# Emptying PSUM banks in steps, adding the residual by DMA, and a fixed TensorE order behind a feed-forward output product

## The chip, the cores and the metric

The kernel is one program on one core of a Trainium2 chip. TensorE (PE) multiplies into eight PSUM banks of 128 x 512 float32; VectorE (DVE), ScalarE (ACT) and GpSimd (POOL) work beside it; SyncE (SP), ACT and POOL issue DMAs. Each engine takes its own instructions in order and waits on semaphores. The metric is the device time of one execution in microseconds, as the median of several runs. Lower is better.

## The reference

Two layers over 256 latent and 256 context tokens, width 1024, all float32. Layer 0 mixes tokens with an mLSTM, layer 1 with latent attention whose keys and values come from a small projection of context and latent tokens together. Behind each mixer comes a convolutional feed-forward block. The part that is changed lies between layer 0's feed-forward and layer 1's attention:

```python
f = _conv_ffn(_modulate(x, ml[3], ml[4]), ...)      # ... (silu(conv(gate)) * up) @ w_out
x = _layer_norm(ALPHA * x + ml[5] * f, ln_g[i, 1], ln_b[i, 1])
# the same for xc with mc; then layer 1:
hl = _modulate(x, ml[0], ml[1])
ckv, k_rope = jnp.split(h @ w_dkv, [A_KVLORA], axis=-1)          # for hc and for hl
kv = _rms_norm(ckv, kv_norm) @ w_ukv
```

## The kernel before, in words

Every float32 product is made of three float32r matmuls (`mm3`, lines 383 to 385): each operand is split into a rounded high part (ACT, line 323 or 388) and a low remainder (DVE, line 326 or 389).

*Weights.* `Stream` holds one list of all weight blocks in the order of use (`_plan`). A block of 128 x 1024 is loaded into a raw buffer (`_load`, by SP), split into a `w` buffer (three of them, `NB`) or, if marked wide, into two `u` tiles, and then used. `use` splits up to eight blocks ahead, as far as `limit` allows and a `w` buffer is free; `pump` does the same up to a given block. A raw buffer becomes free when its block has been split, and then the next load goes out. From block y22 on there are seven raw buffers. Blocks named yt4 are special: SP loads a stored sum (`t2d`, line 278) and POOL adds the weight to it by an accumulating DMA (line 279).

*The output product of layer 0's feed-forward* (`w_fout0`) is a Strassen-like scheme over two token groups (g 0 context, g 1 latent) and two column halves. Four products (yt2, y11, yt3, yt1) run together over six weight blocks and fill all eight PSUM banks (`p6, p1, p7, p5`). Then y21, y22 and yt4 follow, each into one pair of banks (`ps`, one bank for each half b of the 128-row blocks). Operands of the last three are reloaded from DRAM (`zr`, ACT queue) and split (`fz`) by `operand()`. The sums u1 to vv of the four products, gated, are the first part of the output; `add()` adds the gated later products, and bn_stats feed the layer norm. The residual x1 was written to DRAM by `ln_x` two stages earlier and is loaded into `z` (line 1414).

*Order.* A scheduler places the instructions of each engine by the program's order and its own estimate of when each is ready; `keep_in_program_order` (`pin`) holds one instruction behind all earlier ones of its engine. `self.bg` is a list of generators, of which `tick` runs one step.

Before, behind the four products, all banks are emptied at once (lines 1418 to 1434): ACT copies p1 to u1, DVE makes u2, u3, v, u4. `residual()` then multiplies by the gate (1441), adds ALPHA times z (1442), and for the last quarter takes statistics (1444). While yt4's first three blocks run, the context rows are normalised (`z_norm`) and transposed (`ln_T`); then `mid(None, ...)` makes the context's kv product (`mla_ctx`, three dkv blocks held), and only then come yt4's last three blocks (`YTAIL`), wide. The latent rows are normalised and transposed while `ukn` and `uv` use the context's kv; then `mla` begins with the latent kv product and goes on with dq. `PA, PB, PC` limit how far weights are split meanwhile.

Of the kernel before, what the change touches and what calls it, by code (L numbers as in the profile page):

```python
# [11 lines left out]
ALU = mybir.AluOpType  # L12
# [25 lines left out]
PA, PB, PC = 0, 2, 4  # L38
# [32 lines left out]
def _plan():  # L71
# [35 lines left out]
    for n in ("y21", "y22", "yt4"):  # L107
        for j in range(6):
            if (n, j) == ("yt4", 6 - YTAIL):
                for c, m in enumerate((3, 3, 2)):  # L110
                    add(("dkv", 0, c), m * 320)
            add((n, 0, j), cols[j], n == "yt4" and j >= 6 - YTAIL)
    for c in range(2):
        add(("ukn", 0, c), 1024, True)
# [240 lines left out]
class K:  # L355
# [861 lines left out]
    def ln_x(self, ln, zs, dst):  # L1217
# [134 lines left out]
    def w_fout0(self, x1d, mid):  # L1352
# [39 lines left out]
        n = 0  # L1392
        for i in range(6):
            for name, ps, x in (("yt2", p6, "S2"), ("y11", p1, "1"), ("yt3", p7, "S3"), ("yt1", p5, "S1")):
# [7 lines left out]
                if n >= 8:  # L1402
                    operand()
# [6 lines left out]
                if n >= 16 and n % 2 == 0:  # L1410
                    if n == 16:
                        z = []
                    t = self.uf("z")
                    nc.gpsimd.dma_start(t, x1d[len(z)])
                    z.append(t)
                n += 1
        stats = [self.tiny(12, "st").rearrange("p (a b) -> p a b", b=6) for _ in range(4)]
        u1, u3, u4, vv = [], [], [], []
        for b in range(2):
            u = self.s2("u1")  # L1420
            nc.scalar.copy(u, p1[b])
            u1.append(u)
            u = self.s2("u2")
            nc.vector.tensor_tensor(u, p6[b], u1[b], op=ALU.add)
            u4.append(u)
        for b in range(2):
            u = self.s2("u3")
            nc.vector.tensor_tensor(u, p7[b], u4[b], op=ALU.add)
            u3.append(u)
        for b in range(2):  # L1430
            v = self.s2("v")
            nc.vector.tensor_tensor(v, p5[b], u3[b], op=ALU.subtract)
            nc.vector.tensor_tensor(u4[b], p5[b], u4[b], op=ALU.subtract)
            vv.append(v)

        def residual():

            for us, g, c in ((u1, 0, lo), (u4, 0, hi), (u3, 1, lo), (vv, 1, hi)):
                for b in range(2):
                    zz = z[2 * g + b]  # L1440
                    nc.vector.tensor_tensor(us[b], us[b], gate[g][:, c], op=ALU.mult)
                    nc.vector.scalar_tensor_tensor(zz[:, c], zz[:, c], ALPHA, us[b], op0=ALU.mult, op1=ALU.add)
# [528 lines left out]
```

## Time and profile before

| | |
|---|---|
| median of 3 runs (lowest, highest) | 1388.25 us (1387.74, 1389.04) |
| profiled execution, its own time | 1389.13 us |
| span of that profile | 1387.4 us |
| TensorE busy | 1355.8 us, 98% of the span |
| VectorE, ScalarE, GpSimd busy | 77%, 50%, 9% |
| mean granted TensorE clock | 0.997 |
| DMA | 297.63 MB, mean 215 GB/s |

The profile comes from one execution. The span runs from its first to its last instruction; the execution's own time has some microseconds outside it. A busy TensorE is not TensorE at its peak, since matmuls overlap. Idle time of an engine is put down to what ended it; idle time of an engine that bounds nothing costs nothing. In rows of the windows the DMA share is the mean over the core's sixteen DMA engines. Times in rows count from the start of the span.

### The profile page before, as it was taken

The numbers are of one execution on the slowest core, as the hardware profiler recorded it, in microseconds if no ns is written. First come the engines' busy times: TensorE is split into PE (matmuls) and PEld (weight loads), VectorE is DVE, ScalarE is ACT, GpSimd is POOL, SyncE is SP. The second block draws the span as 40 slices with busy tenths as digits, with TensorE's granted clock in tenths as the row PEclk, the third lists the DMA queues.
The fourth block names the chain that finished last, engine by engine and source line by source line (L and its number), as shares of the span: only waits on it lengthen the run. The fifth ranks groups of instructions, "written<-read, shape, count | busy, mean of one in ns | idle before, by whom it ended". The sixth has DMA issues, their size and how long they took to land.

```text
span 1387.4 us, 19172 instructions
## 1 busy us (share of the span) xinstructions
PE 1355.8 (98%) x6903; PEld 1140.1 (82%) x6903; DVE 1075.0 (77%) x1726; ACT 699.2 (50%) x1179; POOL 121.2 (9%) x215
## 2 busy tenths in 40 slices
PE   7999999999999999999999999999999999999997
PEld 3788888888788888878798888888777898899986
DVE  6599757687688697788799878668898789777773
ACT  6585534435444545375643434334547567455560
POOL 0033000011011011120002000000001001000000
PEclk9999999999999999999999999999999999999999
DMA  9689847879666374766747877647987426367750
GB/s 339 217 292 325 289 152 248 237 261 326 210 205 203 104 231 140 242 196 223 242 143 242 295 234 234 211 148 234 310 224 224 137 99 207 116 188 230 209 183 31
DMA packets 97903, 297.63 MB, mean 215 GB/s; under 512 B 12136, under 2 KB 24808, under 8 KB 97808
## 3 DMA queue, kind: packets, MB, share of 16 engines
q1 hardware_dynamic: 68672, 218.52, 48.9%
q0 software_dynamic: 17472, 57.57, 13.4%
q10 hardware_dynamic: 11664, 20.32, 4.0%
q8 instruction: 54, 0.88, 0.3%
q14 instruction: 41, 0.34, 0.1%
HBM read 262.90 MB, written 33.46 MB: 214 GB/s over the span
## 4 chain that ended last, share of the span: by engine, by line
PE 86%; DVE 7%; DMA 3%; ACT 2%; issue 2%; ACTq 0%; SPq 0%; DVEq 0%
PE fin L383 9%; PE fin L384 9%; PE fin L385 9%; PE tok L383 6%; PE tok L385 6%; PE tok L384 6%; PE qk L383 4%; PE qk L384 4%; PE qk L385 4%; PE y L384 4%; PE y L385 4%; PE y L383 4%; PE up L383 2%; PE up L385 2%; PE up L384 2%
## 5 line engine op out<-in xcount | busy, mean ns | idle before, releaser
L326 DVE TENSOR_TENSOR w<-raw,w 128x1024 fp32r<-128x1024 f32 (+3 forms) x290 | 347.9, 1203 | 159.1 <-ACT w L323 158.3
L323 ACT CAST w<-raw 128x1024 fp32r<-128x1024 f32 (+3 forms) x290 | 300.3, 1037 | 331.6 <-PE fin L385 105.0
L384 PE MATMUL fin<-h,w 128*128 128x256 f32 (+1 forms) x696 | 231.7, 333 | 0.0
L385 PE MATMUL fin<-h,w 128*128 128x256 f32 (+1 forms) x696 | 231.4, 333 | 0.0
L383 PE MATMUL fin<-h,w 128*128 128x256 f32 (+1 forms) x696 | 231.2, 333 | 0.1
L512 DVE SCALAR_TENSOR_TENSOR junk<-ar,bc 128x1024 f32<-128x1024 f32 x128 | 155.9, 1218 | 4.9 <-ACT bc L554 2.3
L384 PEld LDWEIGHTS fin<-h,w 128*128 128x128 f32 x696 | 132.2, 190 | 13.0 <-DVE h L1212 0.2
L383 PEld LDWEIGHTS fin<-h,w 128*128 128x128 f32 x696 | 131.9, 190 | 13.2 <-ACT h L1211 0.3
L385 PEld LDWEIGHTS fin<-h,w 128*128 128x128 f32 x696 | 132.2, 190 | 12.7
L383 PE MATMUL qk<-xc,w 128*128 128x512 f32 x256 | 100.7, 393 | 0.0
L385 PE MATMUL qk<-xc,w 128*128 128x512 f32 x256 | 99.9, 390 | 0.0
L384 PE MATMUL qk<-xc,w 128*128 128x512 f32 x256 | 99.8, 390 | 0.0
L383 PEld LDWEIGHTS qk<-xc,w 128*128 128x128 f32 x256 | 48.1, 188 | 10.2 <-issue 0.4
L385 PEld LDWEIGHTS qk<-xc,w 128*128 128x128 f32 x256 | 48.1, 188 | 9.9
L384 PEld LDWEIGHTS qk<-xc,w 128*128 128x128 f32 x256 | 48.1, 188 | 9.6
L383 PE MATMUL up<-hT,w 128*128 128x512 f32 x128 | 50.5, 394 | 0.5 <-ACT hT L388 0.5
L384 PE MATMUL up<-hT,w 128*128 128x512 f32 x128 | 50.1, 392 | 0.4 <-DVE hT L389 0.4
L385 PE MATMUL up<-hT,w 128*128 128x512 f32 x128 | 50.1, 391 | 0.3 <-DVE w L389 0.3
L383 PE MATMUL tok<-w,hT 128*128 128x512 f32 x128 | 49.8, 389 | 0.0
L384 PE MATMUL tok<-w,hT 128*128 128x512 f32 x128 | 49.8, 389 | 0.0
L385 PE MATMUL tok<-w,hT 128*128 128x512 f32 x128 | 49.8, 389 | 0.0
L326 DVE TENSOR_TENSOR wu<-raw,wu 128x1024 fp32r<-128x1024 f32 (+1 forms) x33 | 39.1, 1200 | 8.2 <-ACT wu L323 7.9
(453 smaller groups left out, 3036.6 us busy)
## 6 DMA issues: line engine op xcount, KB each, us to landing
raw<-in_ws SPq DMA_DIRECT2D x287, 512.0 KB, 4.5
ar<-in_adaT SPq DMA_DIRECT2D x80, 512.0 KB, 4.7
adaw<-in_ada_w SPq DMA_DIRECT2D x32, 256.0 KB, 6.5
t2d<-raw ACTq DMA_DIRECT2D x13, 512.0 KB, 6.2
raw<-t2d SPq DMA_DIRECT2D x13, 512.0 KB, 6.3
raw<-in_ws POOLq DMA_DIRECT2D x13, 512.0 KB, 8.0
zr<-fd ACTq DMA_DIRECT2D x33, 128.0 KB, 3.2
xmd<-xr POOLq DMA_DIRECT2D x16, 256.0 KB, 5.4
```

The lines of the kernel that those rows point to most:

```text
L323: k.nc.scalar.copy(h[:, :cols], src)
L326: k.nc.vector.tensor_sub(l[:, :cols], src, h[:, :cols])
L383: mm(out, w[0], x[0], start=start, stop=False)
L384: mm(out, w[0], x[1], start=False, stop=False)
L385: mm(out, w[1], x[0], start=False, stop=stop)
L512: nc.vector.scalar_tensor_tensor(o, w, 1.0, self.bc[j], op0=ALU.mult, op1=ALU.mult, accum_out=col[:, k, j:j + 1])
```

## The change

Six things, all in the stretch described above:

1. u1 is copied from y11's banks right behind y11's last block, pinned, two products before the four end. `operand()` starts at block 6 instead of 8.
2. The sums are made in eight steps of a generator during y21 and y22.
3. x1 is stored already multiplied by ALPHA (`ln_x` has a factor). `z` is no longer loaded: the gated sum is written to it, and a POOL DMA adds x1 to it, half by half, eight of 128 x 512.
4. The dkv blocks stand behind all of yt4 in the list. Weights are split up to them, without PA to PC.
5. yt4's last three blocks follow its first three; between their two halves the context rows are transposed. Then `mla_down`: context kv product, latent transposes, latent kv product, context's ckT, ukn, uv.
6. All TensorE work from yt4 through `mla_down` is issued in the program's order (`manual_schedule`).

The same numbers are computed as before.

```diff
--- before.py
+++ after.py
@@ -35,7 +35,6 @@
 
 AHEAD = 8
 QA, QB, QC = 2, 4, 6
-PA, PB, PC = 0, 2, 4
 
 VE = {1: (3, 0), 2: (3, 0), 3: (3, 0)}
 
@@ -106,10 +105,9 @@
             add((n, 0, j), cols[j])
     for n in ("y21", "y22", "yt4"):
         for j in range(6):
-            if (n, j) == ("yt4", 6 - YTAIL):
-                for c, m in enumerate((3, 3, 2)):
-                    add(("dkv", 0, c), m * 320)
             add((n, 0, j), cols[j], n == "yt4" and j >= 6 - YTAIL)
+    for c, m in enumerate((3, 3, 2)):
+        add(("dkv", 0, c), m * 320)
     for c in range(2):
         add(("ukn", 0, c), 1024, True)
     for c in range(2):
...
@@ -1224,8 +1222,8 @@
         for t in range(2):
             for h in range(2):
                 c = slice(h * 512, (h + 1) * 512)
-                nc.vector.tensor_tensor(zs[t][:, c], zs[t][:, c], g[h], op=ALU.mult)
-                nc.vector.tensor_tensor(zs[t][:, c], zs[t][:, c], b[h], op=ALU.add)
+                nc.vector.scalar_tensor_tensor(zs[t][:, c], zs[t][:, c], scale, g[h], op0=ALU.mult, op1=ALU.mult)
+                nc.vector.scalar_tensor_tensor(zs[t][:, c], b[h], scale, zs[t][:, c], op0=ALU.mult, op1=ALU.add)
                 nc.gpsimd.dma_start(dst[t][:, c], zs[t][:, c])
                 yield
 
...
@@ -1399,7 +1398,7 @@
                         for j in (2 * i, 2 * i + 1):
                             A.pop((f, j), None)
                 self.tick(1)
-                if n >= 8:
+                if n >= 6:
                     operand()
                 if n == 14:
                     gate = []
@@ -1407,57 +1406,62 @@
                         t = self.uf("gate")
                         nc.gpsimd.dma_start(t, self.gd[0, 5][g:g + 1, :].to_broadcast([128, 1024]))
                         gate.append(t)
-                if n >= 16 and n % 2 == 0:
-                    if n == 16:
-                        z = []
-                    t = self.uf("z")
-                    nc.gpsimd.dma_start(t, x1d[len(z)])
-                    z.append(t)
                 n += 1
+                if (name, i) == ("y11", 5):
+                    for b in range(2):
+                        u = self.s2("u1")
+                        pin(nc.scalar.copy(u, p1[b]))
+                        u1.append(u)
         stats = [self.tiny(12, "st").rearrange("p (a b) -> p a b", b=6) for _ in range(4)]
-        u1, u3, u4, vv = [], [], [], []
-        for b in range(2):
-            u = self.s2("u1")
-            nc.scalar.copy(u, p1[b])
-            u1.append(u)
-            u = self.s2("u2")
-            nc.vector.tensor_tensor(u, p6[b], u1[b], op=ALU.add)
-            u4.append(u)
-        for b in range(2):
-            u = self.s2("u3")
-            nc.vector.tensor_tensor(u, p7[b], u4[b], op=ALU.add)
-            u3.append(u)
-        for b in range(2):
-            v = self.s2("v")
-            nc.vector.tensor_tensor(v, p5[b], u3[b], op=ALU.subtract)
-            nc.vector.tensor_tensor(u4[b], p5[b], u4[b], op=ALU.subtract)
-            vv.append(v)
-
-        def residual():
-
-            for us, g, c in ((u1, 0, lo), (u4, 0, hi), (u3, 1, lo), (vv, 1, hi)):
+        z = [self.uf("z") for _ in range(4)]
+
+        def sums():
+
+            def part(us, g, c):
                 for b in range(2):
-                    zz = z[2 * g + b]
-                    nc.vector.tensor_tensor(us[b], us[b], gate[g][:, c], op=ALU.mult)
-                    nc.vector.scalar_tensor_tensor(zz[:, c], zz[:, c], ALPHA, us[b], op0=ALU.mult, op1=ALU.add)
-                    if us is vv:
-                        nc.vector.bn_stats(stats[2 * g + b][:, 1], zz[:, c])
-                    yield
-
-        def add(g, c, ps):
+                    zz = z[2 * g + b][:, c]
+                    nc.vector.tensor_tensor(zz, us[b], gate[g][:, c], op=ALU.mult)
+                    nc.gpsimd.dma_start(zz, x1d[2 * g + b][:, c], accum_op=ALU.add)
             for b in range(2):
+                u = self.s2("u2")
+                nc.vector.tensor_tensor(u, p6[b], u1[b], op=ALU.add)
+                u4.append(u)
+            yield
+            part(u1, 0, lo)
+            yield
+            for b in range(2):
+                u = self.s2("u3")
+                nc.vector.tensor_tensor(u, p7[b], u4[b], op=ALU.add)
+                u3.append(u)
+            yield
+            for b in range(2):
+                v = self.s2("v")
+                nc.vector.tensor_tensor(v, p5[b], u3[b], op=ALU.subtract)
+                vv.append(v)
+            yield
+            for b in range(2):
+                nc.vector.tensor_tensor(u4[b], p5[b], u4[b], op=ALU.subtract)
+            yield
+            part(u4, 0, hi)
+            yield
+            part(u3, 1, lo)
+            yield
+            part(vv, 1, hi)
+            yield
+
+        def add(g, c, ps, bs=(0, 1)):
+            for b in bs:
                 t = self.s2("zp")
                 zz = z[2 * g + b][:, c]
                 nc.vector.tensor_tensor(t, ps[b], gate[g][:, c], op=ALU.mult)
                 nc.vector.tensor_tensor(zz, zz, t, op=ALU.add)
                 nc.vector.bn_stats(stats[2 * g + b][:, c.start // 512], zz)
 
+        self.bg.append(sums())
         ps = pair()
         for i in range(6):
             w = st.use(("y21", 0, i))
             prod(ps, "2", w, i)
-            if i == 1:
-                self.bg.append(residual())
             self.tick(1)
             operand()
         add(0, lo, ps)
@@ -1469,22 +1473,30 @@
             operand()
         self.drain()
         add(0, hi, ps)
-        self.bg = [mid(0, z[0:2], stats[0:2])]
-        self.step(self.bg)
-        ps = pair()
-        for i in range(6 - YTAIL):
-            w = st.use(("yt4", 0, i))
-            prod(ps, "3", w, i)
-            self.tick(2)
-        self.drain()
-        mid(None, None, None)
-        ws = [(i, st.use(("yt4", 0, i), hold=True)) for i in range(6 - YTAIL, 6)]
-        for b in range(2):
-            for i, w in ws:
-                prod(ps, "3", w, i, (b,))
-        st.unhold("yt4")
-        self.fa = self.fd = None
-        self.bg = [mid(1, z[2:4], stats[2:4], lambda: add(1, lo, ps))]
+        self.bg = [self.z_norm(z[0:2], stats[0:2])]
+        with self.tc.manual_schedule(engines={mybir.EngineType.PE}):
+            ps = pair()
+            st.limit = [x[0] for x in st.order].index(("ukn", 0, 0))
+            for i in range(6 - YTAIL):
+                w = st.use(("yt4", 0, i))
+                prod(ps, "3", w, i)
+                self.tick(1)
+                for b in range(2):
+                    if i == 2:
+                        nc.vector.bn_stats(stats[2 + b][:, 1], z[2 + b][:, hi])
+            self.drain()
+            ws = [(i, st.use(("yt4", 0, i), hold=True)) for i in range(6 - YTAIL, 6)]
+            for b in range(2):
+                for i, w in ws:
+                    prod(ps, "3", w, i, (b,))
+                add(1, lo, ps, (b,))
+                if b == 0:
+                    ctx_T(z[0:2])
+            st.unhold("yt4")
+            self.fa = self.fd = None
+            for _ in self.z_norm(z[2:4], stats[2:4]):
+                pass
+            lat(z[2:4])
 
     def z_norm(self, zs, stats):
 
...
@@ -1595,13 +1606,28 @@
                 self.split(u[:, 0], u[:, 1], ps)
                 self.v1.append(u)
 
-    def mla_ctx(self, hc):
-        self.wd = [self.st.use(("dkv", 0, c), hold=True) for c in range(3)]
+    def mla_down(self, hc, latent, hl):
+
+        st = self.st
+        kv0 = [x[0] for x in st.order].index(("ukn", 0, 0))
+        wd = [st.use(("dkv", 0, c), hold=True) for c in range(3)]
         self.ckT = [self.u("ckT0"), self.u("ckT1")]
 
         self.krT = self.u("krT")
         self.nc.vector.memset(self.krT[64:128, 1].bitcast(F32), 0.0)
-        self.dkv_T(self.dkv_rows(self.dkv_mm(hc, self.wd), 0), 0)
+        rows = self.dkv_rows(self.dkv_mm(hc, wd), 0)
+        latent()
+        rows2 = self.dkv_mm(hl, wd)
+        st.unhold("dkv")
+        st.pump(kv0 + 4)
+        self.dkv_T(rows, 0)
+        self.wk = [st.use(("ukn", 0, c)) for c in range(2)]
+        self.wv = [st.use(("uv", 0, c)) for c in range(2)]
+        self.kn = [self.u("kn") for _ in range(H1)]
+        self.v1 = []
+        self.ukn(0)
+        self.rows2 = self.dkv_rows(rows2, 2)
+        self.uv((0, 1))
 
...
@@ -1849,7 +1864,7 @@
             zs = k.zs
             yield from k.ln_T(zs, A, B, dst, g == 1)
             if xdst is not None:
-                k.late.append(k.ln_x(ln, zs, xdst))
+                k.late.append(k.ln_x(ln, zs, xdst, ALPHA if ln == 0 else 1.0))
 
         k.bg = [after0(pc, xr, gate, 0, 0, 0, 3, lambda i: (h0[i][:, 0, 0:256], h0[i][:, 1, 0:256]),
                        [x1d[0], x1d[1]])]
@@ -1881,35 +1896,20 @@
             return lambda i: tuple(us[i // 2][:, n, (i % 2) * 256:(i % 2 + 1) * 256] for n in range(2))
         hc, hl = half(hcu), half(hlu)
 
-        def mid(g, zs, stats, first=None):
-            if g is None:
-                st.limit = kv0 + PA
-                k.rope_load()
-                k.mla_ctx(hc)
-                return
-            return norm1(g, zs, stats, first)
-
-        def norm1(g, zs, stats, first):
-            A, B = k.ln_mod_cols(1, 1, 0, 1 - g)
-            if first is not None:
-                first()
+        def ctx_T(zs):
+            k.rope_load()
+            for _ in k.ln_T(zs, *k.ln_mod_cols(1, 1, 0, 1), hc, False):
+                pass
+
+        def lat(zs):
+            def latent():
                 hlu.extend([k.u("hl") for _ in range(4)])
-            yield from k.z_norm(zs, stats)
-            yield from k.ln_T(zs, A, B, hl if g else hc, g == 1)
-            if g:
-                k.late.append(k.ln_x(1, zs, [x2d[0], x2d[1]]))
-        k.w_fout0(x1d, mid)
+                for _ in k.ln_T(zs, *k.ln_mod_cols(1, 1, 0, 0), hl, True):
+                    pass
+            k.mla_down(hc, latent, hl)
+            k.late.append(k.ln_x(1, zs, [x2d[0], x2d[1]]))
+        k.w_fout0(x1d, ctx_T, lat)
         hc = hcu = None
-        k.tick(1)
-        st.pump(kv0 + PB)
-        k.tick(1)
-        st.pump(kv0 + PC)
-        k.mla_kv()
-        k.ukn(0)
-        k.uv((0,))
-        k.tick(4)
-        k.uv((1,))
-        k.drain()
         k.take_late()
         att = k.mla(hl)
         oT = next(att)
```

More of the change, by code (lines that the diff above doesn't have):

```diff
@@ L1215, in ln_T, with ln_x @@
             yield
-    def ln_x(self, ln, zs, dst):
+    def ln_x(self, ln, zs, dst, scale=1.0):
         nc = self.nc
@@ L1350, in act_sums, with w_fout0 @@
         self.fd.append(d)
-    def w_fout0(self, x1d, mid):
+    def w_fout0(self, x1d, ctx_T, lat):
         nc, st, A = self.nc, self.st, self.fa
@@ L1392, in w_fout0 @@
         n = 0
+        u1, u3, u4, vv = [], [], [], []
         for i in range(6):
@@ L1528, in dkv_mm @@
             hi, lo = hT(k)
-            self.tick(k % 2)
             for t in range(2):
@@ L1611, in rope_load @@
             self.ropet.append((r[:, 0], r[:, 1]))
-    def mla_kv(self):
-        st = self.st
-        self.wk = [st.use(("ukn", 0, c)) for c in range(2)]
-        self.wv = [st.use(("uv", 0, c)) for c in range(2)]
-        self.kn = [self.u("kn") for _ in range(H1)]
-        self.v1 = []
     def mla(self, hl):
@@ L1622, in mla @@
         st.limit = [x[0] for x in st.order].index(("aout", 0, 0))
-        rows = self.dkv_rows(self.dkv_mm(hl, self.wd), 2)
-        self.wd = None
-        st.unhold("dkv")
-        self.tick()
         pss = [self.ps("dq0"), self.ps("dq1")]
@@ L1642, in mla @@
             cq.append(r)
-        self.dkv_T(rows, 2)
+        self.dkv_T(self.rows2, 2)
         self.ukn(1)
```

## The prediction

> **What bounds the kernel now.** I read the page first, then the table of windows, then TensorE's waits, then the DMA queues. Busy shares and slices:
>
> ```profile
> span 1387.4 us, 19172 instructions
> PE 1355.8 (98%) x6903; PEld 1140.1 (82%) x6903; DVE 1075.0 (77%) x1726; ACT 699.2 (50%) x1179; POOL 121.2 (9%) x215
> PEclk9999999999999999999999999999999999999999
> DMA  9689847879666374766747877647987426367750
> ```
>
> TensorE (PE) is the bound: all its idle time is 31.6 us, so only waits can be won. The changed stretch runs from the end of the four first products (about 1002 us) to the first dq product (1089.3 us). Windows, with columns length, busy time per engine, granted clock, DMA share, GB/s:
>
> ```profile
> 1002.00:1089.00 87.00, 79.30 (x402) 66.21 (x403) 80.38 (x147) 49.69 (x90) 9.29 (x14) 0.98 0.68 203
> 1080.00:1085.00 5.00, 4.62 (x21) 4.36 (x22) 5.00 (x13) 3.77 (x11) 0.00 (x0) 0.72 0.00 0
> 1085.00:1090.00 5.00, 5.00 (x33) 5.00 (x32) 4.56 (x7) 2.17 (x5) 2.17 (x4) 0.94 0.63 184
> ```
>
> PE is idle for 87.00 - 79.30 = 7.7 us there, and a low clock loses 5 x 0.28 + 5 x 0.06 = 1.7 us more. So 9.4 us is all that this change can win if it does the same products. Who ends the waits:
>
> ```profile
> engine line waited for: us in total, times, longest us
> PE y L384 <- DVE w L326: 2.1, 2, 1.3
> PE y L383 <- ACT u L1421: 2.0, 1, 2.0
> PE dkv L383 <- ACT hl L1211: 1.5, 1, 1.5
> PE v L384 <- DVE wu L326: 0.8, 2, 0.4
> PE zT L1199 <- DVE z L1500: 0.5, 1, 0.5
> PE dkv L383 <- ACT hc L1211: 0.3, 1, 0.3
> PE kn L385 <- DVE wu L326: 0.2, 1, 0.2
> ```
>
> The first two rows are the banks (the first y21 product waits for the ACT copy of a bank) and VectorE (DVE), which splits weights late because sums and residual fill it. The other resource is DMA, here over the output stage and over its densest 5 us (queue rows: packets, MB, share of 16 engines; issue rows: KB each, median us to landing, 1003 to 1045):
>
> ```profile
> 1002.00:1045.00 43.00, 38.82 (x166) 30.95 (x167) 42.76 (x66) 20.48 (x26) 5.92 (x8) 1.00 0.80 231
> q0 software_dynamic: 179, 0.63, 70.8%
> q1 hardware_dynamic: 177, 0.65, 33.3%
> raw<-t2d SPq DMA_DIRECT2D x5, 512.0 KB, 7.6
> raw<-in_ws POOLq DMA_DIRECT2D x5, 512.0 KB, 8.7
> raw<-in_ws POOLq DMA_DIRECT2D x1, 256.0 KB, 12.8
> ```
>
> DVE is busy 42.76 of 43 us and the DMA engines 80%. Between 1025 and 1030 they are full (70.8% + 33.3%), and in that window q0 carries nothing but the adding DMAs of the yt4 weights (L279). A megabyte that adds cost 0.708 x 5 / 0.63 = 5.6 us of all sixteen engines, a plain one 0.333 x 5 / 0.65 = 2.6 us. The whole forecast rests on this factor of two.
>
> **The change part by part.** Signs are against the profiled execution (1389.13 us, span 1387.4).
>
> *First banks.* The copies of y11's banks are issued two products earlier (2 x 6 matmuls), so y21 finds two free banks. Rows:
>
> ```profile
> 1004.00 0.50 PE L383 MATMUL y<-w,fz 128*128 128x512 f32 x1 [2.04 <-ACT u L1421]
> 1015.33 0.39 PE L385 MATMUL y<-w,fz 128*128 128x512 f32 x1
> 1015.56 0.39 PE L383 MATMUL y<-w,fz 128*128 128x512 f32 x1
> ```
>
> A product costs 0.227 us, so the copies may start 12 x 0.227 = 2.7 us before the four products end. They hold ACT for two times 0.6 us and push the cast of y21's first weights behind them; I leave 0.4 us of the 2.0 us (bounds 0 and 2.0: pinned behind the last zr cast, which waits for its DMA, the copy may be no earlier). Two operand steps move ahead of 1002, where PE has no gap; they take 2 x 0.69 us off DVE in y21.
>
> *Sums in steps, residual by adding DMA.* Each of the eight halves loses its L1442 and keeps the multiply; the two bn_stats of the last quarter (2 x 0.68 us) move into yt4:
>
> ```profile
> L1442 DVE SCALAR_TENSOR_TENSOR z<-z,u x6: 675/680/682, 1012.5 to 1029.9; 128x512 f32<-128x512 f32 x6
> L1414 POOL DMA_DIRECT2D z<-x1d x4: 537/538/540, 953.8 to 975.3; - x4
> L279 POOL DMA_DIRECT2D raw<-in_ws x14: 863/881/1108, 228.6 to 1043.2; - x14
> 950.00:980.00 30.00, 30.00 (x134) 24.86 (x133) 24.83 (x24) 14.70 (x16) 3.23 (x6) 1.00 0.92 311
> ```
>
> DVE is relieved of 8 x 0.68 = 5.4 us in a stretch that it fills, and the sums no longer stand in a block ahead of a split. Both L326 waits (2.1 us) should go. The price is on the DMA engines. Four plain loads of 512 KB go away where PE is busy 30.00 of 30 us, which wins nothing. Eight adding transfers of 256 KB come in at 1005 to 1030: 2.10 MB x 5.6 = 11.8 us of all sixteen engines. POOL issues them (8 x 0.88 us, idle otherwise), each after its DVE multiply, in one line with yt4's adding loads. DVE's add of y21's result now waits for a landing: multiply at about 1006, issue, 8.7 us, so 1016 or 1017, against the end of y21 at 1002.4 + 66 x 0.227 = 1017.4. If late, y22's splits queue behind it; two weights (2 x 2.7 us) are split ahead, which hides up to 5 us. The two rope loads on SP move behind the context's normalisation in the program; they wait for the same two buffers as now and are already in the sum below. ALPHA moves into ln_x: tensor_tensor becomes the L1442 form at the same 0.68 us, nothing.
>
> *dkv behind yt4 (order, limits, mla_down).* Before, the context's transposes and kv product (1045 to 1055.8) lay between yt4's third weight and its last three; PE did other work while those three were still being added up. Now they are wanted at once: after 66 + 66 + 36 products and, with w[3..5] for the first bank, 15 more, so without waits that half ends at 1002.4 + 183 x 0.227 = 1043.9. What DMA has to bring by then, from 1002: what it does now until 1045, 0.80 x 43 = 34.4 us; the residual, 11.8 us; the adding loads of yt4's last three weights, 1.31 MB x 5.6 = 7.3 us, of which 35.0% of 5 us is done by 1045 today:
>
> ```profile
> q0 software_dynamic: 78, 0.32, 35.0%
> ```
>
> so 5.6 us more; less the dkv weights that go behind them, 1.31 MB x 2.6 = 3.4 us. Sum 48.4 us: at a full share the last raw weight lands at 1050.4, and if the dkv loads, issued meanwhile, take their turn, at 1053.8. I take 1052. Cast and split of 512 columns take 1.3 us, the last three products of that bank 0.7 us: 1054.0 instead of 1043.9, a **new wait of 10.1 us** at the yt4 products. From below: the latencies alone (load at about 1025.5, then 7.6 and 8.7 us) give 1041.8 and no wait; from above, if the packets stretch as in the 12.8 us row and the gr/br rows of ln_x share the queue, 1057 and 15 us. On ACT, the square root and normalisation of the context rows and the dkv casts queue behind these casts; they have until after that half.
>
> *Latent next, fixed order.* From there PE does context transposes, yt4's second half, context kv, latent transposes, latent kv, ckT, kn, v in that order, nothing filled in. Rows for the new seams:
>
> ```profile
> 1063.12 0.39 PE L385 MATMUL y<-wu,fz 128*128 128x512 f32 x1
> 1070.45 0.82 ACT L1501 ACTIVATE z<-z,nm,rs 128x512 f32<-128x512 f32 x1 [0.87 <-DVE nm L1499]
> 1048.63 0.42 PE L383 MATMUL dkv<-w,hc 128*128 128x320 f32 x1 [0.32 <-ACT hc L1211]
> 1055.65 0.31 PE L385 MATMUL dkv<-w,hc 128*128 128x320 f32 x1
> 1059.99 0.84 ACT L1563 ACTIVATE ckT<-ckT,sm 128x256 fp32r<-128x256 f32 x2 [2.41 <-PE ckT L1559]
> 1060.50 0.88 DVE L1564 SCALAR_TENSOR_TENSOR ckT<-ckT,sm,ckT 128x256 fp32r<-128x256 f32 x2
> ```
>
> The latent rows are ready 1071.27 - 1063.51 = 7.8 us after the last yt4 product today; the context's kv product covers 1055.96 - 1048.63 = 7.3 us, so 0.5 us stays (bounds 0 and 2, since the ukn and uv splits now sit in the same DVE queue). Latent kv behind its transposes waits as hc does today: 0.3 us instead of 1.5. The evacuation of ckT (1059.99 to 1061.38, 1.4 us for two tiles) was hidden under yt4 products and now stands bare before kn: 0.9 us (bounds 0.4 and 1.4). If the context rows' normalisation comes behind the late casts on ACT, its 0.82 us and the square root before it show partly: 0.5 us (bounds 0 and 2.2). The ukn and uv splits get the time of two kv products, so their waits (0.8 and 0.2 us) go. dq, its weights and everything later keep their order.
>
> *Sum.* -9.4 + 0.4 + 10.1 + 0.5 + 0.3 + 0.9 + 0.5 = +3.3 us: 1392.4 us as a profiled execution. That execution stands 0.88 us above the median of the runs, 1388.25, so the forecast is 1391.5 us, 0.23% slower. From no change this measurement can tell about 0.2%, 2.8 us.
>
> *A rule against the trace.* The two queues fill the engines together in the 1025 to 1030 rows. The Trainium skill, DMA: Bandwidth & Descriptors, section "Issuing engines are not separate DMA queues", says that transfers started by ScalarE, SyncE or GpSimd all run on the same sixteen engines and interleave. By that rule moving the residual to POOL buys no bandwidth and the sum stays as it is; had POOL's transfers engines of their own, the 10.1 us would vanish and the sum be -6.8 us. The trace agrees with the rule (70.8% + 33.3% = 104%).
>
> **The rivals.**
>
> *B. DMA keeps up.* The residual goes out in small pieces early (the DMA share is 0.80 from 1002 to 1045, so a fifth is free), the adds overlap, and the yt4 weights land by the latencies alone. For it: no row of PE's waits names a DMA. Against it: the 104%. Then the wait at yt4 is 0 to 2 us and the sum -6.8 to -4.8: 1381.5 to 1383.5.
>
> *C. Half and half.* The dkv loads yield, and the last weight lands between 1044 and 1050: the wait is 2 to 8 us, the sum -4.8 to +1.2, so 1383.5 to 1389.5. Old waits are traded for one new one.
>
> *D. Later still.* POOL's line is strictly in order: a residual transfer whose DVE multiply is late holds up every adding load of yt4 behind it, and ln_x's rows (1 MB, today 11 to 14 us in that queue) may come before them. It decides from a landing past 1055. Wait 13 to 15 us, sum +6.2 to +8.2: 1394.5 to 1396.5.
>
> *F. The clock falls.* The row of 1080 to 1085, behind the 1.5 us wait on hl, has a clock of 0.72; the row of 1002 to 1045, with the 2.0 us wait in it, has 1.00. One such dip cost 1.7 us (the two window rows), so on top of A it gives 1393.2. The Trainium skill, TensorE: Matmul & The Clock Gate, section "What's actually happening", has the clock fall to half after an idle window of about 3.4 us, the windows running freely. By that rule a wait of 10 us in one piece is certain to bring it. The trace has no wait that long in this stretch, so it shows neither. If the weights land one by one, PE works between them and catches up inside the wait, and the dip costs nothing; I think that likelier.
>
> *E. The early copies are not early.* Pinned behind the last zr casts, they end when they do today: 1.6 us more than the sum, 1393.
>
> **How the numbers follow.** Forecast A (last weight between 1050 and 1055, 1389.5 to 1394.5): 0.40, of which 0.12 lies below 1391.0, the bound of no change. B 0.22, C 0.13 (0.03 of it below 1385.5), D 0.13, E 0.06 (half of it below 1391.0), F 0.06. Faster: 0.22 + 0.03 = 0.25. Within 0.2%: 0.12 + 0.10 + 0.03 = 0.25. Slower: 0.28 + 0.13 + 0.03 + 0.06 = 0.50. The predicted time is A's. The range reaches from B's lower part to D with a dip, 1382 to 1398; it leaves out about 0.08 of B and 0.05 of D. A alone spans 1389.5 to 1394.5.
>
> **What the profile of the changed kernel would show.** First y21 product without the wait on L1421, or with 0.4 us of it. No L326 wait of y products between 1005 and 1030. POOL with eight more issues of about 0.88 us, and the DMA share near 1.0 from 1010 on, with q0 above half of it. If I am right, PE's largest wait is at yt4 products, behind ACT or DVE of a yt4 weight whose adding load landed at 1050 or later, some 10 us in all, and the context's kv product starts near 1060. If that wait is below 2 us, B holds and the factor of two did not bind. zT of the latent rows, latent kv and kn should show 0.5, 0.3 and 0.9 us. What would make the prediction wrong: adding transfers from DRAM rows of 2 KB that cost much less or more than 5.6 us per MB; yt4 loads that start earlier because splits run ahead; or a wait that no row of today shows, of DVE on the residual's landing.

## The result and the profile after

The changed kernel takes 1405.11 us (median of 4 runs, 1404.23 to 1408.14), the kernel before 1387.99 (1387.65 to 1389.04) beside it: ratio 1.0122, 95% interval 1.0109 to 1.0135. It is 17.1 us slower; the forecast was 1391.5, with 1382 to 1398 as its range.

The profiled execution took 1405.34 us. Its busy shares and slices:

```profile
span 1403.4 us, 19160 instructions
PE 1359.0 (97%) x6903; PEld 1143.8 (82%) x6903; DVE 1070.7 (76%) x1718; ACT 699.4 (50%) x1179; POOL 126.5 (9%) x219
PEclk9999999999999999999999999999989999999999
DMA  9689848788665364676747877547894425357650
```

The windows of the changed stretch, columns as before. The first dq product starts at 1104.5 (1089.3 before), so 15.2 of the 16.0 us of longer span lie in here:

```profile
1002.00:1104.50 102.50, 81.06 (x402) 68.34 (x403) 78.09 (x150) 50.05 (x93) 16.57 (x22) 0.92 0.72 200
1030.00:1035.00 5.00, 3.92 (x18) 2.91 (x16) 0.00 (x0) 0.70 (x1) 0.57 (x1) 1.00 1.06 288
1035.00:1040.00 5.00, 0.00 (x0) 0.00 (x0) 0.00 (x0) 0.00 (x0) 2.08 (x3) 0.74 1.07 272
1040.00:1045.00 5.00, 0.00 (x0) 0.00 (x0) 1.07 (x2) 0.00 (x0) 0.88 (x1) 0.50 1.10 219
1045.00:1050.00 5.00, 4.20 (x10) 3.33 (x11) 3.06 (x4) 2.94 (x3) 0.00 (x0) 0.50 1.08 225
1085.00:1090.00 5.00, 2.40 (x13) 1.76 (x12) 5.00 (x12) 3.21 (x11) 0.00 (x0) 0.86 0.94 278
1090.00:1095.00 5.00, 3.80 (x22) 3.29 (x21) 3.25 (x12) 1.36 (x4) 0.00 (x0) 0.80 0.77 283
```

The same 402 products are in the first row as in the 87 us of before. Idle time rose from 7.7 to 102.50 - 81.06 = 21.4 us, busy time by 81.06 - 79.30 = 1.8 us, because matmuls ran at half clock for a while. From 1034.0 to 1043.9 PE, DVE and ACT stand together (POOL only issues DMAs), and the DMA engines are full. TensorE's waits from 1002 to 1105:

```profile
engine line waited for: us in total, times, longest us
PE y L382 <- DVE w L324: 13.5, 3, 11.9
PE kn L381 <- DVE kn L387: 3.8, 4, 1.1
PE zT L1197 <- DVE z L1512: 1.7, 2, 0.9
PE kn L381 <- ACT ckT L1574: 1.0, 1, 1.0
PE kn L382 <- DVE ckT L1575: 0.5, 1, 0.5
PE dkv L383 <- DVE hl L1210: 0.4, 1, 0.4
PE dkv L381 <- ACT hl L1209: 0.4, 1, 0.4
```

They add up to 21.3 us, the idle time. The largest names only the last link. What DVE and ACT stood for is in the waits of all engines from 1002 to 1060, and in their own rows (in brackets the idle time before a row and what ended it):

```profile
DVE st L1486 <- DMA z<-x1d: 16.3, 2, 14.4
ACT wu L321 <- DMA raw<-in_ws: 15.7, 1, 15.7
```

```profile
1043.93 0.69 DVE L1486 BATCH_NORM_STATS2 st<-z 128x6 f32<-128x512 f32 x1 [14.37 <-DMA z<-x1d]
1044.54 1.21 DVE L324 TENSOR_TENSOR w<-raw,w 128x1024 fp32r<-128x1024 f32 x1
...
1046.39 1.04 ACT L321 CAST wu<-raw 128x1024 fp32r<-128x1024 f32 x1 [15.70 <-DMA raw<-in_ws]
1047.35 1.99 ACT L321 CAST w<-raw 128x1024 fp32r<-128x1024 f32 x2
```

PE stood at yt4's first block. Its raw weight had landed at 1027.8, and its split (L324) had one instruction in front of it on DVE: the statistics of the latent rows, which waited for the residual's adding DMA. At the same time ACT stood at the cast of yt4's first *wide* block (wu), ahead of the casts of the second and third block, until that weight landed at 1046.4. Two lines stood for two DMAs.

The DMA queues from 1002 to 1045 and the issues of the adding transfers:

```profile
q0 software_dynamic: 1610, 3.99, 53.1%
raw<-in_ws POOLq DMA_DIRECT2D x5, 512.0 KB, 11.9
z<-x1d POOLq DMA_DIRECT2D x8, 256.0 KB, 12.4
```

q0 carries more than half of the engines' time, and an adding yt4 weight lands 11.9 us after its issue, where it took 8.7.

### The profile page after: what moved, and what is told of

It reads as the page before. It is cut to its first block, busy times and chain, and to the rows that moved or that the text cites. A ratio compares the mean times of both kernels' runs of the same rounds, so it can differ in the third digit from the quotient of the medians.

```text
span 1403.4 us, 19160 instructions
## 1 busy us (share of the span) xinstructions
PE 1359.0 (97%) x6903; PEld 1143.8 (82%) x6903; DVE 1070.7 (76%) x1718; ACT 699.4 (50%) x1179; POOL 126.5 (9%) x219
## 4 chain that ended last, share of the span: by engine, by line
PE 88%; DVE 4%; DMA 3%; ACT 2%; issue 1%; SPq 0%; ACTq 0%; DVEq 0%; POOLq 0%
PE fin L381 9%; PE fin L383 9%; PE fin L382 9%; PE tok L381 6%; PE tok L383 6%; PE tok L382 6%; PE y L382 5%; PE y L383 5%; PE y L381 4%; PE qk L381 4%; PE qk L383 4%; PE qk L382 4%; PE up L381 2%; PE up L383 2%; PE up L382 2%; DMA raw<-in_ws 2%
## 5 line engine op out<-in xcount | busy, mean ns | idle before, releaser
L324 DVE TENSOR_TENSOR w<-raw,w 128x1024 fp32r<-128x1024 f32 (+3 forms) x290 | 348.1, 1203 | 163.0 <-ACT w L321 162.2
L382 PEld LDWEIGHTS fin<-h,w 128*128 128x128 f32 x696 | 132.2, 190 | 13.1 <-DVE h L1210 0.2
L383 PEld LDWEIGHTS fin<-h,w 128*128 128x128 f32 x696 | 132.2, 190 | 12.9
L381 PEld LDWEIGHTS fin<-h,w 128*128 128x128 f32 x696 | 131.9, 190 | 12.9 <-ACT h L1209 0.3
L381 PEld LDWEIGHTS qk<-xc,w 128*128 128x128 f32 x256 | 48.1, 188 | 10.1 <-issue 0.4
L321 ACT CAST wu<-raw 128x1024 fp32r<-128x1024 f32 (+1 forms) x33 | 33.7, 1039 | 23.7 <-DMA raw<-in_ws 23.7
```

What stands on the lines that cost most here:

```text
L321: k.nc.scalar.copy(h[:, :cols], src)
L324: k.nc.vector.tensor_sub(l[:, :cols], src, h[:, :cols])
L381: mm(out, w[0], x[0], start=start, stop=False)
L382: mm(out, w[0], x[1], start=False, stop=False)
L383: mm(out, w[1], x[0], start=False, stop=stop)
```

## The experiments

Every time is a median; the ratio is to the kernel before on the same chips. Theories at the start: **Q**, one DVE instruction stood in front of a split; **B**, adding transfers fill the DMA engines; **S**, the fixed order costs at its seams.

### Statistics out of the way

```diff
-                    if i == 2:
-                        nc.vector.bn_stats(stats[2 + b][:, 1], z[2 + b][:, hi])
...
                 add(1, lo, ps, (b,))
                 if b == 0:
+                    for t in range(2):
+                        pin(nc.vector.bn_stats(stats[2 + t][:, 1], z[2 + t][:, hi]))
```

> Only the two statistics of the latent rows' second half move, from inside yt4's loop to behind the add of yt4's first half, held there. Theory Q (DVE's queue): PE stood 11.9 us at yt4's second block because these statistics waited 14.4 us for the residual's landing, in front of a weight split that was ready. Then yt4's first half is bound by the landing of its last raw weight alone, 1052.7 in the changed kernel, plus 2.0 us for cast, split and three products: 1054.7 instead of 1060.2. Gain 5.5 us, 1399.6 (1398 to 1401.5), and no PE wait above 5 us. Theory B (bandwidth): the adding transfers fill the DMA engines, the last yt4 weight decides whatever DVE does: 1404 to 1405.5. Theory S (the seams of the fixed order behind yt4): 1404 to 1405.5 too.

Measured 1405.60 (ratio 1.0125, 1.0109 to 1.0142): nothing gained. (The text names yt4's second block; in the changed kernel it was the first.) TensorE's waits, and the DVE row behind them:

```profile
PE y L381 <- ACT w L321: 12.5, 1, 12.5
```

```profile
1048.57 1.23 DVE L324 TENSOR_TENSOR wu<-raw,wu 128x1024 fp32r<-128x1024 f32 x1 [15.98 <-ACT wu L321]
```

The first block now goes through; PE stands as long at the second, whose cast is behind ACT's cast of the wide block. Q was half the story.

### Plain residual; adding residual alone; free order

Three runs, each undoing or doing one part:

```diff
 plain residual (z loaded as before, on the changed kernel):
-                    nc.vector.tensor_tensor(zz, us[b], gate[g][:, c], op=ALU.mult)
-                    nc.gpsimd.dma_start(zz, x1d[2 * g + b][:, c], accum_op=ALU.add)
+                    nc.vector.tensor_tensor(us[b], us[b], gate[g][:, c], op=ALU.mult)
+                    nc.vector.tensor_tensor(zz, zz, us[b], op=ALU.add)
 ...
 free order:
-        with self.tc.manual_schedule(engines={mybir.EngineType.PE}):
+        if True:
 ...
 adding residual alone (on the kernel before, with the factor in ln_x):
-                    nc.vector.tensor_tensor(us[b], us[b], gate[g][:, c], op=ALU.mult)
-                    nc.vector.scalar_tensor_tensor(zz[:, c], zz[:, c], ALPHA, us[b], op0=ALU.mult, op1=ALU.add)
...
+                    nc.vector.tensor_tensor(zz, us[b], gate[g][:, c], op=ALU.mult)
+                    nc.gpsimd.dma_start(zz, x1d[2 * g + b][:, c], accum_op=ALU.add)
```

> The changed kernel with four plain loads of the (already scaled) residual as before, and eight tensor adds on DVE in place of the eight adding DMAs; all else as changed. Theories Q and B both: the 11.9 us wait and the half clock behind it (5 x 0.26 + 5 x 0.5 us) go, DVE has 5.4 us more to do: 1405.1 - 14 + 0 to 3 = 1391 to 1394. By B the yt4 weights land 4 us or more earlier than in the changed kernel. Theory S: what stays above 1388.0, about 3 to 6 us, lies behind yt4 (zT, kn, a low clock). If S is nothing: 1383 to 1387.

> The kernel before with the residual by adding DMA alone (eight halves, scaled when stored); the statistics of the latent rows' second half stand behind the last yt4 product. Theory B (an adding MB costs 5.6 us of all engines, 2.10 MB, hence 11.8 us): weights of yt4 and dkv land later, 1391 to 1398. Theory Q (bytes do no harm as long as no DVE instruction waits for a landing in front of a split): 1386 to 1390, since DVE is relieved of 5.4 us and the add of y21 can wait for a landing for some us.

> The changed kernel with TensorE's order from yt4 on left to the planner; all else as changed. Theory Q: the DVE line up to yt4 is the same, the 11.9 us wait stays unless PE finds the context's transposes in between: 1402 to 1406. Theory S (fixed order costs 3 to 6 us at the seams): 1399 to 1402, with the kn and zT waits below 2 us in all.

Measured: plain residual 1398.73 (1.0071, 1.0056 to 1.0086); adding residual alone on the kernel before 1399.22 (1.0075, 1.0060 to 1.0090); free order 1398.16 (1.0067, 1.0052 to 1.0082). So undoing the residual gives 6.4 us and undoing the fixed order 7.0. All three times lie outside the expectations: the first gave back less, the third more, and adding alone cost more than either theory said. The second is not clean: the planner put the statistics ahead of a split again (a DVE wait of 14.4 us for z<-x1d), so it holds the price of the DMA and of the line together. In the run with plain residual, PE still waited 2.9 us for an ACT cast of a yt4 block.

### Both lines held in order

```diff
+            pin = k.tc.keep_in_program_order if key[0] == "yt4" else lambda x: x
-            k.nc.scalar.copy(h[:, :cols], src)
+            pin(k.nc.scalar.copy(h[:, :cols], src))
...
-            k.nc.vector.tensor_sub(l[:, :cols], src, h[:, :cols])
+            pin(k.nc.vector.tensor_sub(l[:, :cols], src, h[:, :cols]))
```

on top of the moved statistics; once with the adding residual, once with the plain one, then the plain one with free order.

> The run with the statistics moved, and beside it the casts (ACT) and splits (DVE) of the six yt4 blocks held in the order of the list. New theory L (two lines): in the changed kernel ACT's cast of yt4's first wide block stands ahead of the casts of yt4's second and third block and waits for its landing at 1046.4; moving the statistics alone left PE standing behind that line. With both lines in order, products start as weights land (1027.8, 1033, 1038.8, 1046.4, 1050.5, 1052.7, each + 1.3): the first half ends at 1054.7 instead of 1060.2, no wait above 5 us, little half clock: 1398 to 1401. Theory B (bandwidth alone): as long as the last weight lands at 1052.7 nothing changes, 1404 to 1406.

> The run with the plain residual, with statistics and yt4's casts and splits held in order. There yt4's raw weights had landed at 1026.5, 1029.0, 1034.5, 1038.7, 1043.4 and 1045.4, y22 ended at 1037.8. Theory L: yt4 then runs through from 1037.8, its first half ends near 1048 instead of 1055: 1390 to 1393, no y wait on ACT. Theory B or S: 1397 to 1399.

> As the run with plain residual and held splits, and TensorE's order from yt4 on left to the planner. Theory S (the fixed order costs at zT, kn and by a low clock near 1085): 3 to 6 us less than that run, 1385 to 1389. If the order is not the cause: the same as that run within 1.5 us.

Measured: 1407.67 (1.0128, 1.0107 to 1.0150), 1401.04 (1.0088, 1.0073 to 1.0103) and 1388.17 (1.0002, 0.9993 to 1.0012). Under the fixed order the held lines gain nothing: the first is 2.1 us above the run with the statistics moved alone, the second 2.3 above the run with plain residual, both outside the expectations. Theory L failed there by its time, but not by its waits. Of the first, the profiled execution took 1401.24 and the three others 1407.5 to 1408.0. In that profile TensorE's waits at y products are 10.3 us, 14.6 with the statistics moved alone. The clock goes with the 6.4 us between the executions: its mean was 0.994 in the profiled one and 0.986 to 0.988 in the others. In the profile it stayed full at kn, though the four waits for kn's split (3.8 us) are those of the changed kernel, where it was 0.86 and 0.80 (windows 1085 to 1095):

```profile
1085.00:1090.00 5.00, 3.00 (x23) 2.60 (x23) 4.70 (x16) 1.79 (x6) 0.00 (x0) 1.00 0.94 325
1090.00:1095.00 5.00, 3.16 (x25) 2.75 (x24) 3.41 (x9) 1.49 (x4) 0.00 (x0) 1.00 0.22 88
```

Where it fell in the three others no trace shows. With free order and a plain residual the time of before is back. So S is large, and what stays of the change (early copies, sums in steps, dkv behind yt4, latent kv next), with the held lines, nets to nothing.

### The residual by itself

The run of 1388.17 again, but with the adding residual; and with the same bytes loaded plainly, written at the head of the sums, and added by DVE:

```diff
 late plain residual:
+            for g, c in ((0, lo), (0, hi), (1, lo), (1, hi)):
+                for b in range(2):
+                    nc.gpsimd.dma_start(z[2 * g + b][:, c], x1d[2 * g + b][:, c])
...
```

> The whole change but the fixed TensorE order, with the statistics behind yt4's first half and yt4's casts and splits held in list order: beside the run with plain residual, held splits and the planner's order (1388.2) only the residual differs. Theory B (adding transfers fill the DMA engines, so that yt4's last weights land some 7 us later, 1052 instead of 1045): 1393 to 1398, a y wait on ACT or DVE of 5 us or more. Theory L alone (all of the loss came from the two lines): 1386.5 to 1389.

> The run with the adding residual, held splits and the planner's order (1395.7), with the same eight halves (2.10 MB) loaded plainly at the head of the sums, and eight adds on DVE. Theory B2 (an adding transfer takes about twice the time of the engines, and comes behind DVE's multiplies): most of the 7.5 us goes, 1387.5 to 1391. Rival B1 (it is the bytes in this stretch, adding or not, that crowd yt4): 1393 to 1397.

Measured: adding 1395.66 (1.0051, 1.0034 to 1.0068), plain and written at the sums 1391.69 (1.0031, 1.0020 to 1.0042), plain and early 1388.17. The queues from 1002 to 1052, first plain and early, then adding (packets, MB, share):

```profile
q1 hardware_dynamic: 2805, 8.98, 52.5%
q0 software_dynamic: 864, 2.88, 32.1%
```

```profile
q0 software_dynamic: 1974, 4.91, 53.2%
raw<-in_ws POOLq DMA_DIRECT2D x5, 512.0 KB, 14.1
```

2.03 MB more on q0 cost 21.1% of 50 us, 10.6 us of all engines, 5.2 us per MB; plain ones on q1 take 0.525 x 50 / 8.98 = 2.9. The last yt4 weight lands at 1053.9 instead of 1046.5: 7.4 us, which is the difference in time (7.5). TensorE waits there:

```profile
PE y L382 <- ACT wu L322: 6.9, 1, 6.9
```

Theory B holds, with both lines in order.

The run of 1391.69 does not load in this stretch. Nothing ties its loads to the sums, and the planner issued them before 1002, much where the early run has its own (961.5 to 982.8). The row, and a TensorE wait from 985 to 1110 that the early run does not have:

```profile
L1428 POOL DMA_DIRECT2D z<-x1d x8: 546/547/555, 974.9 to 985.0; - x8
PE y L382 <- ACT w L322: 2.0, 3, 0.9
```

Between 985 and 996 ACT stood 3.5 us for z<-x1d and 4.3 us for zr<-fd, the operand reloads, and PE was idle 2.6 us longer from 990 to 1010 than in the early run. So its 3.5 us arose in the main before 1010, and the run does not part B2 from B1: how much of the 7.5 us is due to the adding, and how much to any load at this place, stays open.

### The fixed order by itself

The run of 1401.04 (plain, lines held, fixed order), but fixed only up to the latent kv product: the rest of `mla_down` is handed back as a function and called behind the `with` block.

```diff
         st.pump(kv0 + 4)
+
+        def more():
-        self.dkv_T(rows, 0)
+            self.dkv_T(rows, 0)
...
+        return more
...
-            lat(z[2:4])
+            rest = lat(z[2:4])
+        rest()
```

> As the run with plain residual and held splits under the fixed order (1401.0), but the fixed order ends behind the latent kv product: ckT, kn and v are left to the planner. Theory K (the fixed order costs where kn's 48 short products follow ckT at once, waits of 5.2 us and a half clock from 1080 to 1100): 1388 to 1392, clock above 0.9 there. If the cost lies in yt4 and the latent seam: 1397 to 1401.

Measured 1389.34 (1.0006, 0.9997 to 1.0015), 11.7 us less. The windows 1080 to 1095, first fixed throughout, then fixed up to latent kv:

```profile
1080.00:1085.00 5.00, 3.54 (x16) 2.94 (x14) 3.52 (x10) 1.79 (x6) 0.00 (x0) 0.52 0.91 317
1085.00:1090.00 5.00, 3.68 (x15) 3.39 (x16) 3.13 (x12) 0.75 (x2) 0.00 (x0) 0.50 0.27 105
1090.00:1095.00 5.00, 4.08 (x19) 3.69 (x18) 2.65 (x5) 0.97 (x3) 0.47 (x1) 0.50 0.00 0
```

```profile
1080.00:1085.00 5.00, 5.00 (x31) 4.24 (x30) 4.18 (x15) 1.30 (x4) 0.00 (x0) 1.00 0.86 315
1085.00:1090.00 5.00, 5.00 (x30) 4.54 (x30) 3.93 (x9) 2.25 (x6) 1.09 (x2) 1.00 0.13 51
1090.00:1095.00 5.00, 5.00 (x31) 5.00 (x30) 4.83 (x7) 2.62 (x4) 0.00 (x0) 1.00 0.38 111
```

So the loss lies behind latent kv, where ckT, kn and v stand. PE's rows of kn in the changed kernel:

```profile
1087.80 0.28 PE L383 MATMUL kn<-ckT,wu 128*128 128x256 f32 x1
1089.16 0.58 PE L381 MATMUL kn<-ckT,wu 128*128 128x256 f32 x1 [1.08 <-DVE kn L387]
...
1091.68 0.41 PE L383 MATMUL kn<-ckT,wu 128*128 128x256 f32 x1
1093.02 0.39 PE L381 MATMUL kn<-ckT,wu 128*128 128x256 f32 x1 [0.92 <-DVE kn L387]
```

Six products, a wait, twelve products, a wait. `ukn` puts two heads into one bank; the odd head is issued when the even one has been split out of it, and the fixed order leaves PE nothing else to do. If so, another order of heads suffices:

```diff
-        for h in range(H1):
+        pss = {}
+        for h in (0, 2, 1, 3, 4, 6, 5, 7) if g == 0 else range(H1):
...
-                ps = self.ps("kn")
+                pss[h // 2] = self.ps("kn")
+            ps = pss[h // 2]
```

> The changed kernel with one edit: the context's kn products take the heads in the order 0, 2, 1, 3, 4, 6, 5, 7, so that two heads of the same bank never follow each other. Theory P (bank partner): the four kn waits of 1 us (3.8 us) are those of each odd head for the evacuation of the even head in its bank; they go, and the low clock of 1085 to 1095 (1.7 us) with them: 1405.1 - 5.5 = 1398 to 1401. Rival: the waits are for DVE's line, which is late with anything; they stay above 2 us, 1403 to 1406.

> The run with plain residual and held splits under the full fixed order (1401.0), with the same order of heads. Theory P: the 3.7 us of waits and the half clock of 1080 to 1100 (9 us of lost clock in the windows' numbers) go: 1388 to 1391, as where kn was left to the planner (1389.3). Rival: the half clock comes from the zT and ckT waits, not from kn: 1396 to 1400.

Measured: on the changed kernel 1398.62 (1.0077, 1.0062 to 1.0092), 6.5 us less; on the run of 1401.04 it is 1392.11 (1.0029, 1.0018 to 1.0040), 8.9 less and 1.1 above theory P's range. TensorE's wait for kn's split in the first of them:

```profile
PE kn L381 <- DVE kn L387: 0.6, 2, 0.4
```

The row agrees with the Trainium skill, Perfetto Trace Analysis, section "Matmuls", by which independent groups of matmuls should rotate through different banks, so that the evacuation of one overlaps the next: 0.6 us of waits when they do, 3.8 when they don't.

Theory P holds: this one order of heads gives 6.5 of the 7.0 us that free order gives on the changed kernel, and 8.9 of 12.9 us on the run of 1401.04. Of the 6.5 us, 5.1 lie between the first kn product and the first dq product (18.2 us in the changed kernel, 13.1 here): 3.2 are these waits, and the rest goes with the clock (1.00 from 1085 to 1095 instead of 0.86 and 0.80). Where the other 1.4 us lie was not seen.

### Sums in steps

The kernel before with the early copies and the sums in steps alone; then, on it and on the run of 1388.17, the four instructions of the second half's residual one block later:

```diff
             yield
+            yield
             part(u4, 0, hi)
```

> The kernel before with the first two parts alone: u1 copied early and the sums in eight steps (residual by plain loads, multiply and fused add on DVE). If the prediction's steps for them hold (2.0 us wait on the u1 copy down to 0.4, both waits on weight splits, 2.1 us, gone): 1384 to 1386. Rival: two halves' sums and the add of y21 stand in a block of nine DVE instructions ahead of a y22 split, as in the run with the plain residual (3.2 us and a low clock behind it): 1387.5 to 1391.

> The kernel before with the early u1 copies and the sums in steps (1388.9), with the same step one block later. The 3.1 us wait at 1026 and the low clock behind it (0.76 and 0.90 over two 5 us windows, 1.7 us) should shrink to under 1 us: 1384.5 to 1387. Rival: the wait only moves, 1388 to 1390.

> The run with plain residual, held splits and the planner's order (1388.2), with the residual step of the second half (four DVE instructions) one block later, behind y21's add. The 3.2 us wait of y22 behind ten DVE instructions (6 us) and the low clock after it (0.66 over 5 us, 1.7 us) should shrink to under 1 us: 1383.5 to 1386, faster than the kernel before. Rival: the four instructions only move the wait to the next split, 1387.5 to 1389.

Measured: 1388.89 (1.0009, 1.0000 to 1.0019); with the later step 1387.61 (0.9994, 0.9985 to 1.0003); on the other run 1387.99 (0.9999, 0.9990 to 1.0008). The waits for weight splits, without and with the later step:

```profile
PE y L384 <- DVE w L326: 3.4, 2, 3.1
```

```profile
PE y L384 <- DVE w L326: 2.3, 5, 0.8
```

The wait for the copy is gone, but a y22 split stands behind ten DVE instructions, four of the sums and six of y21's add; with the later step its wait falls into small ones. On the kernel before that gives 1.3 us back, between the two expectations; on the other run the wait only moved.

### All repairs together

> The change as a whole with four repairs: plain residual, yt4's casts and splits held in list order, heads in the order of banks, the second half's residual step one block later. If the causes found add up: 1385 to 1388.5, at or a little below the kernel before. If a cause is missing: above 1391.

Measured 1389.66 (1.0010, 1.0000 to 1.0021), between the two expectations. The repairs bring back 15.5 us, nearly all of the loss; no version clearly beats the kernel before.

## Why the prediction was wrong

The direction was right, the size was not. In steps from the changed kernel to one as fast as before: free order 1405.1 to 1398.2 (7.0), both lines in order 1395.7 (2.5), plain residual 1388.2 (7.5). The shares hold for this order of steps: plain residual taken first gave 6.4. By the prediction's own terms, in the changed stretch:

| term | predicted | measured |
|---|---|---|
| all idle time and low clock of before | -9.4 | -9.4 |
| first y21 product | 0.4 | 0.5 |
| y22 splits | 0 | 1.1 |
| yt4 | 10.1 | 11.9 |
| zT, with the late context rows | 1.0 | 1.7 |
| latent kv | 0.3 | 0.8 |
| ckT and kn | 0.9 | 5.3 |
| lost clock (1.7 of before + 1.8) | 0 | 3.5 |
| sum | +3.3 | +15.4 |

*The step that failed* is "The evacuation of ckT ... now stands bare before kn: 0.9 us (bounds 0.4 and 1.4)". Its own part was 1.5 us, just above the upper bound; but behind it the prediction had no term for kn's own banks, and four waits of 3.8 us stood there. It wrote that nothing is filled in and didn't ask what the planner had filled. In the kernel before:

```profile
1063.34 0.28 PE L383 MATMUL kn<-ckT,wu 128*128 128x256 f32 x1
...
1066.82 0.28 PE L385 MATMUL kn<-ckT,wu 128*128 128x256 f32 x1
...
1067.68 0.50 PE L384 MATMUL v<-wu,ckT 128*128 128x512 f32 x1 [0.35 <-DVE wu L326]
...
1069.96 0.40 DVE L389 TENSOR_TENSOR kn<-kn 128x256 fp32r<-128x256 f32 x1
```

Half of kn's 48 products, as many as four heads have, ran before DVE split the first kn bank; the other four heads came from 1070.8 on, one by one between products of v and zT. The order of heads alone gave 6.5 us back, some 5 of them from kn to dq.

*Second, the clock.* Rival F put 1.7 us on it, with 0.06, and A assumed that PE would catch up between weights. The windows show 0.74, 0.50 and 0.50 over the long wait and 0.80 to 0.86 at kn. The trace agrees with the Trainium skill, TensorE: Matmul & The Clock Gate, section "What's actually happening", that a long idle stretch brings half clock; the prediction had cited that and priced it at nothing.

*The adding DMA* was right in its working: 11.8 us of the engines predicted, 10.6 measured; 5.6 us per MB against 5.2; last weight at 1052, and it landed at 1052.7. That the yt4 row comes near, 11.9 against 10.1, is in part luck: in the changed kernel the long wait stood at the first block, behind the two lines, and not at the last weight. With both lines in order the largest wait was 6.9 us, but the time it cost, 7.5 us, stayed below 10.1.

*The lines* of DVE and ACT. The prediction moved two statistics into yt4 and costed them at their own 0.68 us, though for y21's add it had asked what would queue behind it. It named a DVE wait on the residual's landing only as what would make it wrong; it was 16.3 us. That ACT's first wide cast comes ahead of narrow ones was not seen. Together they cost 2.5 us under free order; under the fixed order the median shows no gain from undoing them.

*First banks and splits.* The copy is early, as said (rival E fell). But "both L326 waits should go" did not come true: 1.6 of 2.1 us stayed, since the sums in steps and y21's add stand together ahead of a split.

Rivals B and C fell with the last weight's landing at 1052.7, and so did D, which decided from a landing past 1055. A's landing came true; the time went elsewhere.

## What to carry to other kernels

When a fixed order takes the place of a planner's, walk through the new order bank by bank: a chain that was unbroken because other work lay between may stop at every evacuation. Count an instruction that waits for a DMA at the price of everything behind it on its engine, on every engine that the data passes: removing one of two waits that end together shows nothing. Adding by DMA instead of by VectorE is paid in DMA time, which is dear where weights are due. And look up in the trace when a moved load was issued: where it stands in the program does not fix that.

## What the runs had not been expected to show

- Behind the same four kn waits (3.7 or 3.8 us) the clock differed: 1.00 in the profile with the adding residual and both lines held, 0.86 and 0.80 over two windows in the changed kernel, 0.52, 0.50 and 0.50 over three in the run of 1401.04. Undoing them gave 6.5 us in the second and 8.9 in the third. What decides whether and for how long the half clock comes stays open.
- The planner placed ACT's cast of a wide weight ahead of those of two narrow ones that landed 13.4 and 7.6 us earlier (1033.0, 1038.8 and 1046.4 in the changed kernel), and in the run with the statistics moved again. Why it did was not looked into.
- Eight plain loads of half rows from 974.9 to 985.0 (1391.69) took 3.5 us more than four of whole rows from 961.5 to 982.8 (1388.17). The operand reloads came later, and the last yt4 weight was issued at 1045.1 instead of 1040.1. Which of the two costs the time was not tried.
